# Hybrid encoder on one Trainium2 core: input-projection blocks in another order, the value normalisation's small terms on GpSimd, the convolution's last tile kept in SBUF

## The chip, the cores and the metric

The kernel runs on one core of a Trainium2 chip. The metric is the device time of one execution in microseconds; lower is better. The time before the change is the median of three runs. The hardware profile behind the quoted lines is of one further execution.

A core has five engines that run side by side, each through its own queue in order: TensorE (PE, matrix products; its weight loads are listed as PEld), VectorE (DVE), ScalarE (ACT), GpSimd (POOL) and SyncE (SP), which here only issues transfers. GpSimd issues transfers too: the accumulating ones, which add to a tile in SBUF while they load.

## The reference, cut to what matters

Two layers. Each has a mixer and a gated feed-forward part. The change is in the mixer: one projection, three branches on it, and gates that merge them.

```python
z = xn @ w_in + b_in                       # 1024 positions, 1024 -> 6912
a = zc[..., :768] * sigmoid(zc[..., 768:]) # branch 1
a = dwconv_causal(a, conv_w)               # 31 taps per channel
a = silu(layernorm(a, conv_ln_g, conv_ln_b))
h_a = a @ conv_proj
u, v = split(gelu(zg))                     # branch 2
v = layernorm(v, gmlp_ln_g, gmlp_ln_b)     # then mixed within blocks of 128 positions
h_b = (u * sv) @ gmlp_proj
h_c = multiscale_pool(zp, pool_w, pool_scale) @ pool_proj   # branch 3: windows 2, 4, 8, 16
y = gates[0] * h_a + gates[1] * h_b + gates[2] * h_c        # gates = sigmoid(zgate)
x = x + y @ w_out
```

## The kernel before

**Layout and matrix products.** Channels lie on the 128 partitions, the 1024 positions along the free axis, in two halves of 512. Every float32 operand is split into a rounded part and a remainder (ScalarE casts, VectorE subtracts: `halves`, L343, and `split_to`, L275), and each product is three matmuls of 128x512 (`mms`, L330).

**Blocks.** The input projection has 54 weight tiles of 128 columns. They are taken in pairs, 27 blocks a layer. A block (class `Block`, L364) computes two output tiles `z1` and `z2` over both halves in seven groups of 12 matmuls, a Strassen-like scheme, instead of eight. Its activation operands (`B11`, `B21`, `T2`, `T3`, `T1`, `T4`, `B22`, four buffers each, 28 in all) are made once per layer in `start_phase` (L496) and held through the whole projection. The weight sums that the scheme needs (`s1` to `s4`) are made by accumulating transfers on GpSimd's queue (`more`, L212, and `prepare`, L223), begun nine operands ahead of use. Plain weights (`raw`) are loaded by SyncE, and weights are split three operands ahead (`operand`, L295). `Block.rest` (L392) takes the last four groups: `s3` with `T3`, `s1` with `T1`, plain weights with `T4`, `s4` with `B22`.

**Kinds of blocks.** `glu` blocks give the convolution branch's inputs, `v` and `u` the two parts of branch 2, `zp` the pooling branch, `gate` the gates. `IN_BLOCKS` (L81) is their order, written out by hand. The first four (`EARLY`) share the start phase.

**Background work.** A finished block can append jobs to `background`: a `glu` block one convolution tile (`conv_taps`, L585: 30 steps of one tap on VectorE, and one to sum up the tiles for all but the first), a `v` block two transposed tiles (`transposed`, L646: two steps each), a `zp` block two pooling tiles (`pool_windows`, L607: three to six steps each). `u` and `gate` blocks append nothing; they store their two tiles to DRAM. `pump` (L313) takes a step of the first two jobs in turn. It is called six times a block (four for the first four blocks), with 1.4 steps a call, and 1.8 in the last six blocks. This order is the program's; a planner that places the instructions on the engines' queues at compile time may move them ahead of or behind it, as buffers and its own estimates allow.

**Buffers.** Nearly all tiles of 128x1024 float32 (512 KB, and the operands of the same size) come from one pool of 37 (`slot` and `wide`, L113 and L117). A tile that is stored to DRAM keeps its buffer until the store has landed.

**After the projection.** `mixer_out` (L723) loads the pooled tiles back (`load_pooled`, L714, two transfers of 512 KB each; three of the six tiles in the last block, L701, the others in the loop of L748), mixes them (`mix`), and then runs branch 2 (`spatial`, L769), the convolution's normalisation (`conv_mean`, L823, `conv_norm`, L849) as background work of the three branch projections (`branch`, L873). `spatial` takes the mean and variance of `v` from statistics (`bn`), and makes two tiles of 128x4: `rv`, the inverse root of the variance (an addition on VectorE, L781, and the power on GpSimd, L782), and `nm`, minus the mean times `rv` (VectorE, L784). ScalarE applies them (L786). `conv_mean` loads the six convolution tiles and their sum back from DRAM.

Of the kernel before, what the change touches and what calls it, by code (L numbers as in the profile page):

```python
# [13 lines left out]
P = 128  # L14
# [62 lines left out]
N_PAR = C_LAST + KD  # L77


GATE_BLOCKS = [("gate", j) for j in range(N_GATE // 2)]  # L80
IN_BLOCKS = (  # L81
# [3 lines left out]
    + [("glu", 3)] + GATE_BLOCKS[0:3]  # L85
    + [("glu", 4)] + GATE_BLOCKS[3:6]
    + [("glu", 5)] + GATE_BLOCKS[6:12]
)
EARLY = 4
KEEP = 4  # L90
# [11 lines left out]
def encoder(ctx: ExitStack, tc: tile.TileContext, xt, wts, par, bs, wst, cnt, out):  # L102
# [24 lines left out]
    def half(h):  # L127
        return slice(h * H, (h + 1) * H)
# [184 lines left out]
    def pump(n):  # L313

        state["credit"] = state["credit"] + n if background else 0
        while state["credit"] >= 1 and background:
            job = background.pop(0)
            try:
                next(job)
                state["credit"] -= 1  # L320
                background.insert(1, job)
            except StopIteration:
                pass
# [37 lines left out]
    def add(o, a, b, op=ALU.add):  # L361
        nc.vector.tensor_tensor(o, a, b, op=op)  # L362

    class Block:  # L364
# [24 lines left out]
            self.u2 = temp(f"u2_{self.name}")  # L389
            nc.scalar.copy(self.u2, self.run)  # L390

        def rest(self, dst21, dst22, n_pump=0):  # L392

            key, ops, run, u2 = (self.l, self.ta, self.tb), self.ops, self.run, self.u2
            ps = pm.tile([P, H], F32, tag="mm", name=f"c21_{self.name}")
            mms(ps, operand("s3", key), ops["T3"], True, True)
            p7 = temp(f"p7_{self.name}")
            nc.scalar.copy(p7, ps)  # L398
            pump(n_pump)
            mms(run, operand("s1", key), ops["T1"], False, True, again=True)  # L400
            add(dst22, p7, run, ALU.subtract)
            pump(n_pump)
            mms(ps, operand("raw", (self.l, self.tb, H)), ops["T4"], False, True, again=True)
            add(dst21, ps, u2, ALU.subtract)
            pump(n_pump)
            mms(run, operand("s4", key), ops["B22"], False, True, again=True)
            pump(n_pump)
            return run
# [157 lines left out]
    def mixer_in(l, x0, x1, sq1, ops):  # L566
# [1 line left out]
        tag = f"{l}"  # L568
        d = {
            "gate": [dp.tile([P, S], F32, name=f"gate_{l}_{i}") for i in range(N_GATE)],  # L570
            "conv": [dp.tile([P, S], F32, name=f"convd_{l}_{i}") for i in range(KB)],
            "pooled": [],
            "csum": dp.tile([P, S], F32, name=f"csumd_{l}"),
            "bn": lay.tile([P, S // BLK, KB, 6], F32, tag="bn", name=f"bn_{l}"),
            "u": [dp.tile([P, S], F32, name=f"ud_{l}_{i}") for i in range(KB)],
            "v": dp.tile([P, S // BLK, DB], F32, name=f"vd_{l}"),
# [8 lines left out]
        def conv_taps(i, ain):  # L585
            acc = wide(f"conv_{tag}_{i}")
            w0 = C_CW + i * CONV_K + CONV_K - 1
            nc.scalar.activation(acc, ain, AF.Copy, bias=0.0, scale=col(w0))  # L588
            for k in range(1, CONV_K):
                nc.vector.scalar_tensor_tensor(  # L590
                    acc[:, k:], ain[:, : S - k], col(w0 - k), acc[:, k:],
                    op0=ALU.mult, op1=ALU.add,
                )
                yield
            nc.sync.dma_start(d["conv"][i], acc)

            if i == 0:
                conv_sum.append(acc)
                return
            total = wide(f"csum_{tag}_{i}")  # L600
            add(total, conv_sum.pop(), acc)
            conv_sum.append(total)
            if i == KB - 1:
                nc.sync.dma_start(d["csum"], total)
            yield

        def pool_windows(i, z):  # L607
# [59 lines left out]
        def rest(n, b, n_pump):  # L667
            kind, j = IN_BLOCKS[n]
            z1, z2 = b.z, wide(f"z2_{b.name}")
            ps = b.rest(z2[:, half(0)], z2[:, half(1)], n_pump)  # L670
            if kind == "glu":
                pointwise(z1, ps, AF.Sigmoid, C_BB + j)
                nc.vector.scalar_tensor_tensor(
                    z2, z2, col(C_BA + j), z1, op0=ALU.add, op1=ALU.mult
                )
                background.append(conv_taps(j, z2))
                return
            func, bias = {
                "v": (AF.Gelu_apprx_tanh, C_BV), "u": (AF.Gelu_apprx_tanh, C_BU),
                "zp": (AF.Identity, C_BP), "gate": (AF.Sigmoid, C_BG),  # L680
            }[kind]
            pointwise(z1, ps, func, bias + 2 * j)
            pointwise(z2, None, func, bias + 2 * j + 1)
            for i, z in enumerate((z1, z2)):
                c = 2 * j + i
                if kind == "v":
                    background.append(transposed(c, z))
                elif kind == "zp":
                    background.append(pool_windows(c, z))
                else:  # L690
                    nc.sync.dma_start(d[kind][c], z)
# [31 lines left out]
    def mixer_out(l, d, x_src, x_dst):  # L723
# [45 lines left out]
        def spatial(h):  # L769
# [8 lines left out]
                nc.vector.bn_aggr(mv[:, b, :], d["bn"][:, h * NB + b])  # L778
            yield
            rv = sm.tile([P, NB], F32, tag="rv", name=f"rv_{tag}_{h}")  # L780
            nc.vector.tensor_scalar(rv, mv[:, :, 1], EPS, None, op0=ALU.add)  # L781
            nc.gpsimd.tensor_tensor(rv, rv, mhalf, op=ALU.pow)  # L782
            nm = sm.tile([P, NB], F32, tag="nm", name=f"nm_{tag}_{h}")
            nc.vector.scalar_tensor_tensor(nm, mv[:, :, 0], -1.0, rv, op0=ALU.mult, op1=ALU.mult)  # L784
            for b in range(NB):
                nc.scalar.activation(  # L786
                    v[b][:, :DB], v[b][:, :DB], AF.Identity,
# [33 lines left out]
        conv, squares = [], []  # L821

        def conv_mean():  # L823
            acc = wide(f"csum_{tag}_b")
            reload(acc, d["csum"])
            for i in range(KB):
                c = wide(f"convn_{tag}_{i}")
                reload(c, d["conv"][i])
                conv.append(c)
            yield  # L830
            for h in range(NH):
                sl = half(h)
                mean = pst.tile([P, H], F32, tag="st", name=f"mean_{tag}_{h}")
                nc.tensor.matmul(mean, ones, acc[:, sl], start=True, stop=True)
                sq = None
                for i in range(KB):
                    nc.vector.scalar_tensor_tensor(
                        conv[i][:, sl], mean, -1.0 / DB, conv[i][:, sl], op0=ALU.mult, op1=ALU.add
                    )
                    s = temp(f"csq_{tag}_{h}_{i}")  # L840
                    nc.scalar.activation(s, conv[i][:, sl], AF.Square)
                    if sq is None:
                        sq = s
                    else:
                        add(sq, sq, s)
                    yield
                squares.append(sq)
# [46 lines left out]
                    pump(n_pump)  # L894


        for h in range(NH):
            background.insert(h, spatial(h))
        background.append(conv_mean())
        branch(2, mixed, PUMP[1])  # L900
        drain()
        background.append(conv_norm())
# [289 lines left out]
```

## Time and profile before

| | us |
|---|---|
| median of 3 runs | 2734.74 |
| lowest and highest run | 2734.66, 2737.49 |
| the profiled execution, its own time | 2737.02 |
| its span, first to last instruction | 2735.2 |
| PE busy in the span | 2678.3 |
| DVE busy | 2059.5 |
| ACT busy | 1254.3 |
| POOL busy | 360.6 |

A line of the timeline gives the start, the length, the engine, the line of the kernel, the operation, what it writes `<-` what it reads, the shape, and how many instructions are merged (x12). In square brackets stands how long the engine was idle before it, and what released it. Matmuls are pipelined: the length of a group runs to the modelled end of its last one, so distances between starts are the better measure. A line of the waits gives who waited `<-` for whom: the total in us, how often, and the longest. In a line of stretches the stretch and its length come first, then each engine's busy time, the granted TensorE clock as a share of full speed, the DMA engines' share and GB/s.

In the profiled execution the projection ends and the loop of `mix` begins at 563.5 us in the first layer and at 1907.8 us in the second.

### The profile page before, as it was taken

The page shows a single profiled execution, that of the slowest core. Times are in us where ns is not written, and L with a number is a line of the kernel's source. Part 1 is how long each engine was busy: PE and PEld are TensorE (multiplying, and loading weights), DVE is VectorE, ACT ScalarE, POOL GpSimd, SP SyncE. Part 2 cuts the span into 40 slices and gives each one's busy share as a digit, 9 for nine tenths or more (in the row PEclk, how much of TensorE's full clock was granted, in tenths as well). Part 3 has the DMA queues.
Part 4 walks back from the last instruction along what each step waited for, and adds up shares of the span by engine and source line. Part 5 has one row for each costly group of instructions (what it writes and reads, how often), then busy time and mean ns, then how long its engine had stood idle before and what let it go on. Part 6 is the DMA issues. An engine that isn't in the chain of part 4 may idle for free. (4 is left out here: it accounts for less than half of the span.)

```text
span 2735.2 us, 35037 instructions
## 1 busy us (share of the span) xinstructions
PE 2678.3 (98%) x12122; PEld 2208.2 (81%) x12122; DVE 2059.5 (75%) x2887; ACT 1254.3 (46%) x2047; POOL 360.6 (13%) x411
## 2 busy tenths in 40 slices
PE   6999999999999999999999999999999999999998
PEld 4887888888888788878888878888788888888788
DVE  7988989867756876674579878988676579666656
ACT  5554444443333554453364444444452336445534
POOL 2212111100001221100122111110000022111000
PEclk9999999999999999999999999999999999999999
DMA  9887787684357787665568777876724677774654
GB/s 240 198 216 187 201 230 202 173 281 164 122 177 204 166 209 177 172 203 197 150 149 212 205 206 216 210 208 198 272 81 137 221 181 179 201 182 115 216 179 137
DMA packets 275075, 517.92 MB, mean 189 GB/s; under 512 B 28496, under 2 KB 49744, under 8 KB 274896
## 3 DMA queue, kind: packets, MB, share of 16 engines
q1 hardware_dynamic: 220272, 415.51, 45.8%
q0 software_dynamic: 54624, 100.16, 22.2%
q8 instruction: 95, 1.56, 0.2%
q14 instruction: 84, 0.69, 0.1%
HBM read 385.54 MB, written 89.13 MB: 174 GB/s over the span
## 5 line engine op out<-in xcount | busy, mean ns | idle before, releaser
L287 DVE TENSOR_TENSOR split<-raw,split 128x512 fp32r<-128x512 f32 (+1 forms) x570 | 376.9, 665 | 245.8 <-ACT split L286 238.4
L286 ACT CAST split<-raw 128x512 fp32r<-128x512 f32 (+1 forms) x570 | 342.7, 603 | 465.2 <-PE ph L336 152.3
L590 DVE SCALAR_TENSOR_TENSOR conv<-z_glu,par,conv 128x1017 f32<-128x1017 f32 (+9 forms) x360 | 452.3, 1263 | 10.9 <-ACT conv L588 8.3
L286 ACT CAST split<-s 128x512 fp32r<-128x512 f32 x344 | 213.3, 622 | 363.7 <-issue 120.2
L336 PE MATMUL pd<-h,split 128*128 128x512 f32 (+1 forms) x1536 | 315.1, 364 | 3.4 <-ACT split L286 1.5
L336 PEld LDWEIGHTS pd<-h,split 128*128 128x128 f32 x1536 | 261.9, 188 | 52.0 <-ACT h L358 3.4
L287 DVE TENSOR_TENSOR split<-s,split 128x512 fp32r<-128x512 f32 x344 | 234.9, 686 | 68.2 <-ACT split L286 67.9
L218 POOL DMA_DIRECT2D s<-in_wts_dram x220 | 204.3, 971 | 424.7 <-DMA s<-in_wts_dram 183.6
L218 POOL DMA_DIRECT2D s<-s x156 | 135.9, 871 | 762.5 <-DMA s<-in_wts_dram 290.6
L336 PE MATMUL run_up<-T_f,split 128*128 128x512 f32 x768 | 184.5, 389 | 2.5 <-ACT T_f L345 2.5
L336 PE MATMUL c_up<-T_f,split 128*128 128x512 f32 x768 | 183.8, 389 | 0.3 <-ACT p_up L398 0.3
L336 PE MATMUL run_up<-B_f,split 128*128 128x512 f32 x768 | 182.0, 391 | 2.1 <-DVE upv L362 2.1
L336 PE MATMUL po<-y,split 128*128 128x512 f32 x768 | 175.7, 389 | 0.0
L336 PEld LDWEIGHTS run_up<-B_f,split 128*128 128x128 f32 x768 | 143.4, 188 | 34.2 <-DVE upv L362 4.4
L336 PEld LDWEIGHTS run_up<-T_f,split 128*128 128x128 f32 x768 | 143.8, 188 | 33.4 <-ACT T_f L345 3.4
L336 PEld LDWEIGHTS c_up<-T_f,split 128*128 128x128 f32 x768 | 144.0, 188 | 31.0 <-ACT p_up L398 1.2
L336 PEld LDWEIGHTS po<-y,split 128*128 128x128 f32 x768 | 144.0, 188 | 29.8
L336 PE MATMUL run_gate<-T_m,split 128*128 128x512 f32 x576 | 138.4, 389 | 0.0
L336 PE MATMUL c_gate<-T_m,split 128*128 128x512 f32 x576 | 138.3, 389 | 0.0
L336 PE MATMUL run_gate<-B_m,split 128*128 128x512 f32 x576 | 136.0, 390 | 0.1
L336 PE MATMUL ph<-mixed,split 128*128 128x512 f32 x576 | 135.4, 393 | 0.0
L336 PE MATMUL ph<-us,split 128*128 128x512 f32 x576 | 134.2, 391 | 0.0
(256 smaller groups left out, 4378.3 us busy)
## 6 DMA issues: line engine op xcount, KB each, us to landing
raw<-in_wts_dram SPq DMA_DIRECT2D x518, 256.0 KB, 3.3
s<-in_wts_dram SPq DMA_DIRECT2D x344, 256.0 KB, 3.7
s<-in_wts_dram POOLq DMA_DIRECT2D x220, 256.0 KB, 5.3
s<-s POOLq DMA_DIRECT2D x156, 256.0 KB, 4.2
gate<-z_gate SPq DMA_DIRECT2D x48, 512.0 KB, 4.3
gt<-gate SPq DMA_DIRECT2D x96, 256.0 KB, 3.6
h<-hd SPq DMA_DIRECT2D x56, 256.0 KB, 4.6
pooled_b<-poold SPq DMA_DIRECT2D x24, 512.0 KB, 8.0
```

The lines of the kernel that those rows point to most:

```text
L218: nc.gpsimd.dma_start(s, o, accum_op=ALU.add)
L286: nc.scalar.copy(s[:, 0, :cols], src[:, :cols])
L287: nc.vector.tensor_tensor(s[:, 1, :cols], src[:, :cols], s[:, 0, :cols].bitcast(F32), op=ALU.subtract)
L336: nc.tensor.matmul(ps[:, cols], w[:, i0, wsl], a[:, i1, cols], start=first and k == 0 and j == 0, stop=last and k == n - 1 and j == 2, ski ...
L590: nc.vector.scalar_tensor_tensor(acc[:, k:], ain[:, : S - k], col(w0 - k), acc[:, k:], op0=ALU.mult, op1=ALU.add,)
```

## The change

It has four parts.

1. `IN_BLOCKS` is put in another order. The number and the kinds of blocks are the same. The third `v` block moves into the first four, the three `zp` blocks move back to positions 8, 12 and 16 (from 3, 6 and 9), and the first six gate blocks, which stood three by three behind `glu` 3 and 4, are spread over positions 4, 6, 14, 15, 18 and 19 (counted from 0).
2. In `spatial`, `rv`'s addition and `nm`'s product move from VectorE to GpSimd; `nm`'s one instruction becomes two.
3. `Block.rest` gets a callback `freed`, called after its first, second and third group. In the last block it loads one more pooled tile each time, so that all six are loaded within that block.
4. The last convolution tile and the sum of the tiles stay in SBUF, where they were stored to DRAM and loaded back. `conv_mean` waits for the sum by yielding. `spatial` is appended to the background list where it was inserted at its front.

```diff
+GATES = [("gate", j) for j in range(N_GATE // 2)]
 IN_BLOCKS = (
-    [("glu", 0), ("v", 0), ("v", 1), ("zp", 0)]
-    + [("glu", 1), ("v", 2), ("zp", 1), ("u", 0)]
-    + [("glu", 2), ("zp", 2), ("u", 1), ("u", 2)]
-    + [("glu", 3)] + GATE_BLOCKS[0:3]
-    + [("glu", 4)] + GATE_BLOCKS[3:6]
-    + [("glu", 5)] + GATE_BLOCKS[6:12]
+    [("glu", 0), ("v", 0), ("v", 1), ("v", 2), GATES[0]]
+    + [("glu", 1), GATES[1], ("u", 0), ("zp", 0)]
+    + [("glu", 2), ("u", 1), ("u", 2), ("zp", 1)]
+    + [("glu", 3), GATES[2], GATES[3], ("zp", 2)]
+    + [("glu", 4), GATES[4], GATES[5]]
+    + [("glu", 5)] + GATES[6:12]
 )
...
-        def rest(self, dst21, dst22, n_pump=0):
+        def rest(self, dst21, dst22, n_pump=0, freed=None):
+            freed = freed or (lambda: None)
...
             mms(ps, operand("s3", key), ops["T3"], True, True)
             p7 = temp(f"p7_{self.name}")
             nc.scalar.copy(p7, ps)
+            freed()
             pump(n_pump)
             mms(run, operand("s1", key), ops["T1"], False, True, again=True)
             add(dst22, p7, run, ALU.subtract)
+            freed()
             pump(n_pump)
             mms(ps, operand("raw", (self.l, self.tb, H)), ops["T4"], False, True, again=True)
             add(dst21, ps, u2, ALU.subtract)
+            freed()
             pump(n_pump)
...
-            "conv": [dp.tile([P, S], F32, name=f"convd_{l}_{i}") for i in range(KB)],
+            "conv": [dp.tile([P, S], F32, name=f"convd_{l}_{i}") for i in range(KB - 1)],
-            "csum": dp.tile([P, S], F32, name=f"csumd_{l}"),
...
-            nc.sync.dma_start(d["conv"][i], acc)
+            if i < KB - 1:
+                nc.sync.dma_start(d["conv"][i], acc)
...
             if i == KB - 1:
-                nc.sync.dma_start(d["csum"], total)
+                d["conv_last"], d["csum"] = acc, total
...
-            ps = b.rest(z2[:, half(0)], z2[:, half(1)], n_pump)
+            freed = (lambda: load_pooled(l, d)) if n == len(IN_BLOCKS) - 1 else None
+            ps = b.rest(z2[:, half(0)], z2[:, half(1)], n_pump, freed)
...
-            nc.vector.tensor_scalar(rv, mv[:, :, 1], EPS, None, op0=ALU.add)
+            nc.gpsimd.tensor_scalar(rv, mv[:, :, 1], EPS, None, op0=ALU.add)
             nc.gpsimd.tensor_tensor(rv, rv, mhalf, op=ALU.pow)
             nm = sm.tile([P, NB], F32, tag="nm", name=f"nm_{tag}_{h}")
-            nc.vector.scalar_tensor_tensor(nm, mv[:, :, 0], -1.0, rv, op0=ALU.mult, op1=ALU.mult)
+            nc.gpsimd.tensor_tensor(nm, mv[:, :, 0], rv, op=ALU.mult)
+            nc.gpsimd.tensor_scalar(nm, nm, -1.0, None, op0=ALU.mult)
...
         def conv_mean():
-            acc = wide(f"csum_{tag}_b")
-            reload(acc, d["csum"])
-            for i in range(KB):
+            for i in range(KB - 1):
                 c = wide(f"convn_{tag}_{i}")
                 reload(c, d["conv"][i])
                 conv.append(c)
             yield
+            while "csum" not in d:
+                yield
+            conv.append(d["conv_last"])
+            acc = d["csum"]
...
-        for h in range(NH):
-            background.insert(h, spatial(h))
-        background.append(conv_mean())
+        background.extend([spatial(0), spatial(1), conv_mean()])
```

More of the change, by code (lines that the diff above doesn't have):

```diff
@@ L77 @@
 N_PAR = C_LAST + KD
-GATE_BLOCKS = [("gate", j) for j in range(N_GATE // 2)]
+GATES = [("gate", j) for j in range(N_GATE // 2)]
 IN_BLOCKS = (
[3 rows of a table removed]
-    + [("glu", 3)] + GATE_BLOCKS[0:3]
-    + [("glu", 4)] + GATE_BLOCKS[3:6]
-    + [("glu", 5)] + GATE_BLOCKS[6:12]
+    [("glu", 0), ("v", 0), ("v", 1), ("v", 2), GATES[0]]
[4 more added lines that the diff above has]
+    + [("glu", 5)] + GATES[6:12]
 )
```

## The prediction

> **What bounds the kernel now.** I read the head of the page first, then TensorE's waits, then the stretches around the places that this list names.
>
> ```profile
> span 2735.2 us, 35037 instructions
> PE 2678.3 (98%) x12122; PEld 2208.2 (81%) x12122; DVE 2059.5 (75%) x2887; ACT 1254.3 (46%) x2047; POOL 360.6 (13%) x411
> ...
> PE st_m L416 <- DVE sq_m L362: 13.2, 1, 13.2
> PE run_u L336 <- DVE z_u L362: 8.3, 2, 4.3
> PE mix L336 <- DMA pooled_b<-poold: 2.8, 3, 1.6
> PE sv L797 <- ACT v L786: 0.4, 1, 0.4
> ```
>
> TensorE (PE) is busy 98% of the span, so only 56.9 us of idle time can be won at all, plus whatever its clock loses. The change removes no matmul. The largest wait, st_m at the kernel's start, lies ahead of everything it touches. What it can reach are the run_u and mix waits. The run_u wait comes once per layer:
>
> ```profile
> 250.51 0.61 PE L336 MATMUL c_u<-B_m,split 128*128 128x512 f32 x2
> 255.38 5.49 PE L336 MATMUL run_u<-B_m,split 128*128 128x512 f32 x12 [4.25 <-DVE z_u L362]
> 260.66 2.64 PE L336 MATMUL c_u<-B_m,split 128*128 128x512 f32 x10
> 263.14 2.88 PE L336 MATMUL run_u<-T_m,split 128*128 128x512 f32 x12
> 265.86 2.88 PE L336 MATMUL c_u<-T_m,split 128*128 128x512 f32 x12
> ...
> 1595.21 0.61 PE L336 MATMUL c_u<-B_m,split 128*128 128x512 f32 x2
> 1599.85 5.49 PE L336 MATMUL run_u<-B_m,split 128*128 128x512 f32 x12 [4.03 <-DVE z_u L362]
> 1607.78 2.88 PE L336 MATMUL run_u<-T_m,split 128*128 128x512 f32 x12
> ```
>
> Twelve matmuls take 2.72 us here (263.14 to 265.86). The twelve after the gap took 5.28 (255.38 to 260.66): half speed. So count the loss from start to start: from 250.51 twenty-four matmuls should end 5.44 later, at 255.95; the next group began at 263.14, so 7.19 us are lost, of which 4.25 are idle. In layer 1 it is 1607.78 - (1595.21 + 5.44) = 7.13. Together 14.3 us, although the list of waits shows only 8.3. The granted clock confirms it:
>
> ```profile
> 80.00:231.40 151.40, 151.40 (x689) 125.41 (x688) 140.52 (x210) 77.70 (x123) 30.79 (x35) 1.00 0.83 205
> 231.40:276.70 45.30, 41.05 (x170) 33.40 (x169) 30.05 (x47) 19.21 (x34) 10.13 (x10) 0.92 0.74 202
> 447.50:563.50 116.00, 116.00 (x513) 96.10 (x512) 104.68 (x118) 50.32 (x79) 14.05 (x16) 1.00 0.70 196
> ```
>
> The columns are length, then PE, weight load, VectorE (DVE), ScalarE, GpSimd (POOL), the clock (1.00, in the gap's stretch 0.92) and DMA. Before the gap DVE is busy 140.5 of 151.4 us, 93%, and PE never waits. DVE has little slack there, and what makes it wait is soon passed on to PE.
>
> The Trainium skill, "TensorE: Matmul & The Clock Gate", Part 1, says that the clock falls to half after an idle window of some 3.4 us and returns after as long a busy one. By it a gap costs its idle time and 1.7 us more (half of 3.4): an estimate of 11.7 us for both. The trace's 2.94 and 3.10 beyond the idle time decide.
>
> **Why DVE was late.** DVE's timeline before the late z_u additions, both layers:
>
> ```profile
> 240.31 1.22 DVE L362 TENSOR_TENSOR win<-win 128x1022 f32<-128x1022 f32 x1
> ...
> 242.46 0.16 DVE L784 SCALAR_TENSOR_TENSOR nm<-mv,rv 128x4 f32<-128x4 f32 x1 [0.93 <-POOL rv L782]
> 247.17 0.17 DVE L784 SCALAR_TENSOR_TENSOR nm<-mv,rv 128x4 f32<-128x4 f32 x1 [2.42 <-POOL rv L782]
> 252.89 1.23 DVE L362 TENSOR_TENSOR win<-z_zp 128x1023 f32<-128x1023 f32 x1 [2.33 <-DMA poold<-pooled]
> 254.64 0.68 DVE L362 TENSOR_TENSOR z_u<-p_u,run_u 128x512 f32<-128x512 f32 x1
> ...
> 1587.82 0.17 DVE L784 SCALAR_TENSOR_TENSOR nm<-mv,rv 128x4 f32<-128x4 f32 x1 [0.94 <-POOL rv L782]
> 1591.85 0.16 DVE L784 SCALAR_TENSOR_TENSOR nm<-mv,rv 128x4 f32<-128x4 f32 x1 [1.73 <-POOL rv L782]
> 1597.38 1.22 DVE L362 TENSOR_TENSOR win<-z_zp 128x1023 f32<-128x1023 f32 x1 [2.13 <-DMA poold<-pooled]
> ```
>
> DVE waited 0.93 + 2.42 + 2.33 = 5.68 us for a 4.25 us gap on PE, and 0.94 + 1.73 + 2.13 = 4.80 us for 4.03. So PE absorbs 0.8 to 1.4 us and gets the rest. Two causes stand side by side: the round trip to GpSimd's power, and a pooling window that waits for a buffer until the store of a pooled tile has landed.
>
> **The change, part by part.** *Value terms on GpSimd.*
>
> ```profile
> L786 ACT ACTIVATE v<-v,nm,rv x16: 1011/1014/1030, 591.6 to 1945.0; 128x768 f32<-128x768 f32 x16
> L781 DVE TENSOR_SCALAR rv<-mv x4: 93/136/165, 240.3 to 1588.6; 128x4 f32<-128x4 f32 x4
> L782 POOL TENSOR_TENSOR rv<-rv,mhalf x4: 1352/1644/1947, 240.5 to 1590.5; 128x4 f32<-128x4 f32 x4
> L138 POOL MEMSET mhalf<- 128x4 f32 x1 | 0.1, 102 | 0.0
> ```
>
> The planner has moved rv and nm some 350 us ahead of their reader (first starts 240.3 and 591.6), into the middle of the input projection. The edit takes 4 rv and 4 nm off DVE: 4 x 0.14 + 4 x 0.16 = 1.2 us busy, and above all the waits, 3.35 us in layer 0 and 2.67 in layer 1. GpSimd gets three instructions more per half, 12 in all, each between 0.10 us (its memset of the same shape) and 1.64 us (its power): 1.2 to 19.7 us in all. I take about 0.3 each, near the memset, since plain arithmetic isn't a power. Behind them in GpSimd's queue stand the accumulating DMAs of the weight sums; one half can hold them back by 0.3 to 4.9 us. GpSimd is busy 10.1 of 45.3 us there and the sums are begun nine operands (9 x 2.72 = 24 us) before use, so I cost that at nothing; without that cover it is at most 4.9 us per half.
>
> A rule speaks against the move: the Trainium skill, "GPSIMD Engine Reference", section 1, says that GpSimd shares its SBUF interface with VectorE and that instructions with two SBUF inputs contend. What that would do is a rival below.
>
> *Order of the blocks.* No block is added or dropped; the total of background steps is the same (185 convolution, 12 value, 28 pooling steps), and both orders leave one step at the end. What changes is how many 512 KB buffers of the shared pool of 37 are held. Stepping through pump() for both orders, with 28 held by the projection's operands: the old order wants 38 at blocks 7, 8, 10, 11 and 13 (counted from 0), and the gap is at the end of block 10, where a window waits for a buffer. The new order wants at most 37, at blocks 4 (the old order wants 37 there as well) and 18, where the last pooling tiles now are, and 33 to 36 elsewhere. The count leaves out how long stores hold a buffer:
>
> ```profile
> poold<-pooled SPq DMA_DIRECT2D x12, 512.0 KB, 5.1
> gate<-z_gate SPq DMA_DIRECT2D x48, 512.0 KB, 4.3
> csumd<-csum SPq DMA_DIRECT2D x2, 512.0 KB, 3.3
> csum_b<-csumd SPq DMA_DIRECT2D x2, 512.0 KB, 6.3
> ```
>
> So at block 18 a wait between 0 and 5.1 us (a whole store) is possible. I take about 1, under what PE absorbs, since the old order's waits came only above 37. With both causes gone, both gaps go: 14.3 us. Next late is nothing that the list of waits shows in this stage.
>
> *Loads of the pooled tiles into freed operand buffers.*
>
> ```profile
> 568.13 4.50 SPq L201 DMA_DIRECT2D pooled_b<-poold  x6
> ...
> 563.52 9.68 PE L336 MATMUL mix<-pooled_b,split 128*128 128x512 f32 x42
> 573.99 0.93 PE L336 MATMUL mix<-pooled_b,split 128*128 128x512 f32 x3 [0.78 <-DMA pooled_b<-poold]
> 575.34 9.12 PE L336 MATMUL mix<-pooled_b,split 128*128 128x512 f32 x39 [0.42 <-DVE mixed L759]
> ...
> 1919.10 0.93 PE L336 MATMUL mix<-pooled_b,split 128*128 128x512 f32 x3 [1.59 <-DMA pooled_b<-poold]
> 1920.45 9.09 PE L336 MATMUL mix<-pooled_b,split 128*128 128x512 f32 x39 [0.42 <-DMA pooled_b<-poold]
> ...
> DMA to landing us min/median/max: 4.9/8.7/11.0
> ```
>
> Six loads (three tiles) go out at 568.13 for matmuls that were due at 573.2. The edit puts them behind the last block's T3, T1 and T4 groups: mix begins at 563.52, three groups of 2.72 after T3's end, so from about 555.4 on. With 11.0 us to land they are there by about 569. Waits removed: 0.78 + 1.59 + 0.42 = 2.8 us; the 0.42 for DVE stays. The price: SyncE's queue waits for those groups, and the weight loads for mix queue behind by at most one group, 2.72 us; they are split several us ahead of use, so nothing. Bounds of this part: 3.2 us gained to 5.4 lost.
>
> *Last convolution tile and sum in SBUF.* Per layer two stores and two loads of 512 KB go. No PE wait names them, so nothing is gained. Two buffers stay held until conv_mean; the value loads could come later, and PE's one wait for them is 0.4 us. Bounds: 0.4 gained, 3.3 (a store's time) lost per layer; I take 0. The changed place of spatial() in the background list does nothing, as the list is empty by then.
>
> **The sum.** 14.3 + 2.8 = 17.1 us. The profiled execution took 2737.02 us, 1.8 more than its span; it becomes about 2719.9, the span 2718.1. The median of the runs before, 2734.74, is 0.08% under the profiled one, and becomes 2717.6. The three runs spread over 2.8 us, so 0.2% (5.5 us) is about what can be told from no change.
>
> **Rivals.**
> *Half of it:* GpSimd's round trip goes but the buffer wait stays. PE's gaps shrink to 4.25 - 3.35 = 0.90 and 4.03 - 2.67 = 1.36 us. A gap of 1.59 us (at 1919.10) was followed by full speed, so no clock is lost: 2.3 us more, 2719.9. This lies inside my own range.
> *The gap moves:* the static order puts an equal stall elsewhere in each layer, likeliest at blocks 17 to 19, where 37 of 37 buffers are wanted and two gate stores of 4.3 us each lie between. Price 14.3 us: 2731.9, no difference that can be told. For it: DVE is 90% busy in the last blocks (104.7 of 116). Against: there, too, PE never waited. That the edits leave the waits where they are comes to the same time. Chance 0.17.
> *Slower:* both pooling tiles of that pair wait for a store at the same place, behind gate stores in SyncE's queue; each holds DVE a whole 5.1 us, and the faster tap rate of the last six blocks leaves no slack between. Each stall is then about a gap of 4 us and 3 us of half clock. Four such cost 28.6: 2746.2. It decides against the change from 17.1 us, 8.6 per layer. For it: that pair has moved next to those blocks. Against: the old order's pair ran beside gate blocks as well, and PE's list of waits names no z_gate. Chance 0.10.
> *GpSimd slows DVE:* if DVE stands still while the 12 added instructions run at their upper 1.64 us, and PE sees all of it, 19.7 us return: 2737.3, within 0.2%. Against: the window addition that ran beside the first power (both start at 240.3 to 240.5) took 1.22 us, and those with no power beside them 1.22 and 1.23 (252.89, 1597.38). Chance 0.03, shared between same and slower.
>
> **How the numbers follow.** Forecast with the half case 0.70, its own range 2714 (the remaining 0.4 + 0.4, and the spread) to 2722 (half case plus 2). To 2736 the range takes in the moved gap and leaves out the slower case and edges, under 0.2. Faster by over 0.2% (under 2729.3): 0.70. Same: 0.17 and part of the last, 0.18. Slower: 0.12.
>
> **What would show it.** Right: no run_u or other PE wait over 2 us between 80 and 565 us and in the same part of layer 1, the clock 1.00 throughout; no DVE wait for POOL rv; mix without a pooled_b wait. Wrong: a PE wait for a z_ addition at another block, a DVE win wait over 2 us at blocks 16 to 19, or s sums landing late behind GpSimd's new instructions.

## The result, and the profile after

| | before | after |
|---|---|---|
| first comparison, median us (runs) | 2736.11 (4) | 2721.73 (4) |
| second comparison, the same kernel again | 2733.84 (9) | 2718.73 (5) |
| ratio, 95% interval: first | | 0.9943 [0.9932, 0.9955] |
| ratio, 95% interval: second | | 0.9944 [0.9931, 0.9956] |
| profiled execution, span | 2735.2 | 2719.7; second one 2714.3 |

The change makes the kernel faster by 0.57%, about 15.5 us; the interval allows 12 to 19. The forecast was 17.1 us, and the time forecast, 2717.6, stands 1.1 us below the second median and 4.1 below the first.

The head of the page after the change, with its busy times, and the line of PE's waits that has grown:

```profile
PE 2671.9 (98%) x12122; PEld 2206.4 (81%) x12122; DVE 2058.4 (76%) x2879; ACT 1254.6 (46%) x2047; POOL 370.2 (14%) x423
...
PE sv L806 <- ACT v L795: 2.1, 3, 1.1
```

The lines for run_u on z_u and for mix on pooled_b are gone; the one for sv (branch 2 mixing the values `v`, which come back from DRAM, over positions) has grown from 0.4 to 2.1. DVE's busy time is 1.1 us less and POOL's 9.6 more. (Line numbers have shifted: L336 is now L337, L782 now L790.) PE's timeline where the gap of layer 0 was, and the first two stretches again, around that place:

```profile
245.67 2.88 PE L337 MATMUL c_u<-T_m,split 128*128 128x512 f32 x12
248.39 5.60 PE L337 MATMUL run_u<-B_m,split 128*128 128x512 f32 x24
253.83 2.88 PE L337 MATMUL c_u<-B_m,split 128*128 128x512 f32 x12
```

```profile
80.00:231.40 151.40, 151.40 (x690) 125.36 (x689) 142.59 (x214) 76.14 (x120) 37.47 (x42) 1.00 0.83 211
231.40:276.70 45.30, 45.30 (x201) 37.53 (x200) 32.91 (x40) 23.88 (x37) 7.91 (x9) 1.00 0.84 231
```

Twenty-four matmuls take 5.44 us, start to start (248.39 to 253.83). PE is busy throughout both stretches at clock 1.00. In the first stretch POOL has 6.7 us more than before, since the value terms of both halves now lie there. The mix follows without a gap (the first nine of its 84 matmuls already stand ahead of the projection's last group, at 553.03), and the new wait comes behind it:

```profile
557.89 17.16 PE L337 MATMUL mix<-pooled_b,split 128*128 128x512 f32 x75
574.89 12.40 PE L337 MATMUL ph<-mixed,split 128*128 128x512 f32 x54
...
588.74 1.94 PE L806 MATMUL sv<-ws,v 128*128 128x128 f32 x18 [0.78 <-ACT v L795]
```

```profile
1927.54 1.94 PE L806 MATMUL sv<-ws,v 128*128 128x128 f32 x18 [1.12 <-ACT v L795]
```

**A ruler for the stage.** Whole times scatter by several us from run to run, so the kernels are also compared by one stretch of PE's timeline: the last 2150 matmuls ahead of the first `ph` (the branch projections) of a layer, counted one by one in the trace, from about 91 us to the end of mix in layer 0 and the same in layer 1. Before the change they took 492.93 us in layer 0 and 493.31 in layer 1. After it they took 482.92 in both, in the second profile 482.93 and 482.91. So 10.0 + 10.4 = 20.4 us went. The stretch from the first `ph` to the first `po` (the product with `w_out`) grew by 1.08 and 1.02 (213.39 to 214.47, 214.26 to 215.28), in the second profile by 0.07 and not at all.

The rest of the difference between the spans lies in code that the change does not touch. The feed-forward's first product of layer 0 (first `run_up` to first `pd`) took 310.52 us before, 312.33 and 310.18 in the two profiles after, and 309.5 to 312.8 over all the kernels below. The matmuls of layer 0 ahead of the ruler, from the first `run_glu` on, took 70.68 before, 70.99 and 71.14 after, and 70.6 to 74.5 below. One run of the kernel with the loads alone, 3361.23 us at a granted clock of 0.753 where its other runs had 0.995 to 0.997, lies far off all others and is left out of its ratio.

### The profile page after: what moved, and what is told of

Read it like the earlier page. It is cut to its first block, busy times and chain, and to the rows that moved or that the text cites. A ratio compares the mean times of both kernels' runs of the same rounds, so it can differ in the third digit from the quotient of the medians.

```text
span 2719.7 us, 35012 instructions
## 1 busy us (share of the span) xinstructions
PE 2671.9 (98%) x12122; PEld 2206.4 (81%) x12122; DVE 2058.4 (76%) x2879; ACT 1254.6 (46%) x2047; POOL 370.2 (14%) x423
## 4 chain that ended last, share of the span: by engine, by line
PE 81%; issue 13%; DVE 3%; DMA 2%; ACT 1%; POOL 0%; SPq 0%; DVEq 0%; POOLq 0%; ACTq 0%
PE run_up L337 13%; PE pd L337 12%; PE run_gate L337 10%; PE c_up L337 9%; PE c_gate L337 7%; PE run_glu L337 5%; PE ph L337 4%; PE c_glu L337 4%; PE po L337 3%; PE run_zp L337 2%; PE run_u L337 2%; PE run_v L337 2%; PE c_u L337 2%; PE c_zp L337 2%; PE c_v L337 1%
## 5 line engine op out<-in xcount | busy, mean ns | idle before, releaser
L595 DVE SCALAR_TENSOR_TENSOR conv<-z_glu,par,conv 128x1011 f32<-128x1011 f32 (+7 forms) x360 | 452.5, 1264 | 7.3 <-ACT conv L593 4.5
L337 PE MATMUL pd<-h,split 128*128 128x512 f32 (+1 forms) x1536 | 314.7, 364 | 3.7 <-ACT split L287 1.5
L337 PEld LDWEIGHTS pd<-h,split 128*128 128x128 f32 x1536 | 262.2, 189 | 51.9 <-ACT h L359 3.5
L337 PE MATMUL run_up<-T_f,split 128*128 128x512 f32 x768 | 184.5, 389 | 2.5 <-ACT T_f L346 2.5
L337 PE MATMUL run_up<-B_f,split 128*128 128x512 f32 x768 | 183.4, 393 | 2.5 <-DVE upv L363 2.5
L337 PE MATMUL c_up<-T_f,split 128*128 128x512 f32 x768 | 183.8, 389 | 0.3 <-ACT p_up L401 0.3
L337 PE MATMUL po<-y,split 128*128 128x512 f32 x768 | 175.7, 389 | 0.0
L337 PEld LDWEIGHTS run_up<-B_f,split 128*128 128x128 f32 x768 | 144.2, 189 | 34.8 <-DVE upv L363 4.7
L337 PEld LDWEIGHTS run_up<-T_f,split 128*128 128x128 f32 x768 | 143.8, 188 | 33.4 <-ACT T_f L346 3.5
L337 PEld LDWEIGHTS c_up<-T_f,split 128*128 128x128 f32 x768 | 144.0, 188 | 31.1 <-ACT p_up L401 1.2
L337 PEld LDWEIGHTS po<-y,split 128*128 128x128 f32 x768 | 144.0, 188 | 29.8
L337 PE MATMUL c_gate<-T_m,split 128*128 128x512 f32 x576 | 138.6, 389 | 0.0
L337 PE MATMUL run_gate<-T_m,split 128*128 128x512 f32 x576 | 138.5, 389 | 0.0
L337 PE MATMUL run_gate<-B_m,split 128*128 128x512 f32 x576 | 136.3, 389 | 0.0
L337 PE MATMUL ph<-mixed,split 128*128 128x512 f32 x576 | 136.1, 394 | 0.0
L337 PE MATMUL ph<-us,split 128*128 128x512 f32 x576 | 134.2, 391 | 0.0
```

Of the source, the lines that this page charges most:

```text
L337: nc.tensor.matmul(ps[:, cols], w[:, i0, wsl], a[:, i1, cols], start=first and k == 0 and j == 0, stop=last and k == n - 1 and j == 2, ski ...
L595: nc.vector.scalar_tensor_tensor(acc[:, k:], ain[:, : S - k], col(w0 - k), acc[:, k:], op0=ALU.mult, op1=ALU.add,)
```

## Experiments

The four parts are called order, GpSimd, loads and SBUF. Each table row gives the median, the ratio to the kernel before in its own comparison, and the ruler. The kernel before had 2737.17 us in the comparison with the four parts alone, 2734.21 in that with the two kernels that leave out SBUF or the loads, and 2733.84 in that of the other rows.

| parts in the kernel | us | ratio [95%] | last 2150 matmuls, L0 / L1 |
|---|---|---|---|
| none (before) | | 1 | 492.93 / 493.31 |
| GpSimd | 2729.50 | 0.9970 [0.9959, 0.9981] | 487.86 / 488.05 |
| order | 2729.43 | 0.9976 [0.9967, 0.9986] | 489.68 / 487.41 |
| loads | 2732.71 | 0.9981 [0.9972, 0.9990] | 489.61 / 490.04 |
| SBUF | 2733.84 | 0.9987 [0.9978, 0.9997] | 491.67 / 490.11 |
| order, GpSimd | 2720.56 | 0.9954 [0.9942, 0.9967] | 484.75 / 484.25 |
| GpSimd, loads, SBUF | 2724.19 | 0.9960 [0.9946, 0.9973] | 486.28 / 486.53 |
| order, GpSimd, loads | 2718.89 | 0.9951 [0.9938, 0.9963] | 482.92 / 482.91 |
| order, GpSimd, SBUF | 2718.41 | 0.9949 [0.9936, 0.9963] | 483.70 / 483.70 |
| all | 2718.73 | 0.9944 [0.9931, 0.9956] | 482.93 / 482.91 |

(In the kernels with SBUF and without loads the planner sets four `mean` matmuls ahead of the first `ph`, inside the ruler. Each takes 0.43 us where the others take 0.23; take 0.8 us off there.)

### GpSimd alone

```diff
-            nc.vector.tensor_scalar(rv, mv[:, :, 1], EPS, None, op0=ALU.add)
+            nc.gpsimd.tensor_scalar(rv, mv[:, :, 1], EPS, None, op0=ALU.add)
...
-            nc.vector.scalar_tensor_tensor(nm, mv[:, :, 0], -1.0, rv, op0=ALU.mult, op1=ALU.mult)
+            nc.gpsimd.tensor_tensor(nm, mv[:, :, 0], rv, op=ALU.mult)
+            nc.gpsimd.tensor_scalar(nm, nm, -1.0, None, op0=ALU.mult)
```

> The kernel before with the value terms on GpSimd alone; order, loads and stores as before. If both causes add up (my theory): the DVE waits for POOL rv go, the wait for poold stays, PE's gap shrinks from 4.25 and 4.03 us to about 0.9 and 1.4 with the clock staying at 1.00: 12 us faster than before, about 2724. If the buffers decide and the round trip to GpSimd is harmless: the gaps stay over 3 us with the clock dip, no difference, 2736. If the round trip alone makes the gap: no gap over 0.3 us, 14.3 us faster, 2722.

The gaps shrank to 2.14 and 2.25 us, not to 0.90 and 1.36. DVE's and PE's timelines of this kernel at the place:

```profile
247.70 0.69 DVE L287 TENSOR_TENSOR split<-s,split 128x512 fp32r<-128x512 f32 x1 [1.32 <-ACT split L286]
250.88 1.23 DVE L362 TENSOR_TENSOR win<-z_zp 128x1023 f32<-128x1023 f32 x1 [2.49 <-DMA poold<-pooled]
```

```profile
250.60 0.61 PE L336 MATMUL c_u<-B_m,split 128*128 128x512 f32 x2
253.36 3.03 PE L336 MATMUL run_u<-B_m,split 128*128 128x512 f32 x12 [2.14 <-DVE z_u L362]
256.23 2.43 PE L336 MATMUL c_u<-B_m,split 128*128 128x512 f32 x10
```

DVE no longer waits for GpSimd, and the window addition starts at 250.88 instead of 252.89: 2.01 us earlier, where 3.35 us of waits had gone. The freed time met two other waits. The split waits 1.32 us for ScalarE (0.17 before), and the store's landing, which the window waits for, came late enough to make that wait 2.49 instead of 2.33. 3.35 - 1.15 - 0.16 = 2.04. The gap on PE shrank by the same, 4.25 - 2.14 = 2.11. And after a gap of 2.14 us the next twelve matmuls took 2.87 (253.36 to 256.23): no half clock. The ruler gained 5.07 and 5.26.

### Order alone

```diff
-    [("glu", 0), ("v", 0), ("v", 1), ("zp", 0)]
-    + [("glu", 1), ("v", 2), ("zp", 1), ("u", 0)]
...
+    [("glu", 0), ("v", 0), ("v", 1), ("v", 2), GATES[0]]
+    + [("glu", 1), GATES[1], ("u", 0), ("zp", 0)]
...
```

> The kernel before with the new order of blocks alone; rv and nm stay on VectorE. If both causes add up: no DVE wait for poold, but the wait for the power remains, some 3 to 4 us, now at an earlier block; PE absorbs 0.8 to 1.4 of it and shows a gap of 2 to 3 us without loss of clock: 14.3 - 2 x 2.5 = 9 us faster, about 2727. If the order alone decides: no gap, 14 us faster, 2722. If the round trip alone makes the gap: it moves with nm, over 3.4 us with the clock dip, no difference, 2736.

No window waits for a store in this kernel, and there is no gap at run_u. New gaps stand at another block, 80 us earlier. GpSimd, DVE and PE:

```profile
163.60 0.88 POOL L218 DMA_DIRECT2D s<-s  x1 [6.93 <-DMA s<-in_wts_dram]
164.16 2.36 POOL L782 TENSOR_TENSOR rv<-rv,mhalf 128x4 f32<-128x4 f32 x2
```

```profile
165.57 0.16 DVE L784 SCALAR_TENSOR_TENSOR nm<-mv,rv 128x4 f32<-128x4 f32 x1 [5.54 <-POOL rv L782]
166.55 0.16 DVE L784 SCALAR_TENSOR_TENSOR nm<-mv,rv 128x4 f32<-128x4 f32 x1 [0.82 <-POOL rv L782]
```

```profile
169.24 3.01 PE L336 MATMUL run_gate<-T_m,split 128*128 128x512 f32 x12 [2.29 <-ACT u_gate L390]
172.09 2.88 PE L336 MATMUL c_gate<-T_m,split 128*128 128x512 f32 x12
176.62 3.06 PE L336 MATMUL run_gate<-B_m,split 128*128 128x512 f32 x12 [1.66 <-DVE z_gate L362]
```

With the third `v` block in the first four, the statistics are complete at some 160 us instead of 240, and the planner sets the value terms there. At that point an accumulating DMA on GpSimd's queue is waiting 6.93 us for the load that it adds to. The power stands behind it in order, and DVE stands 5.54 us behind the power. Both powers together take 2.36 us once they run; it isn't the power that is slow. So the order by itself trades one stall of DVE for another; the ruler gained 3.25 and 5.90.

### Order and GpSimd together, and everything but the order

The first kernel has the two diffs above. The second has GpSimd, loads and SBUF, with the old `IN_BLOCKS`.

> Only the new order and the GpSimd edit. Theory (the gap needs both, and they do not add): no wait of PE at a z_u, u_gate or z_gate addition over 1 us between 80 and 565 us or in the same part of layer 1, so the whole 14.3 us go, where the two singly brought 7 to 8 us each and left gaps of 1.7 to 2.3 us. The waits of mix on its pooled tiles stay (before: 0.78 + 0.42 in layer 0, 1.59 + 0.42 in layer 1) because the store of the sum still stands in SyncE's queue: about 2 to 3 us over the kernel with all parts, 2720 to 2724. Rival (the loads or the kept sum take part in removing the gap): a gap of 1 us or more stays at one of these places, 2724 or more.

> All parts but the new order of the blocks. Theory (the order is needed for what the GpSimd edit leaves): the wait of VectorE's window addition for the store of a pooled tile stays, with a gap of PE of about 2.1 and 2.3 us at run_u as in the kernel with the GpSimd edit alone; mix does not wait. About 4.4 us over the kernel with all parts: 2724 to 2727. Rival (the old order is as good once GpSimd has the value terms and the sum stays in SBUF): no gap over 1 us, time within 2 us of the kernel with all parts.

With both, PE has no wait between 80 us and the mix of layer 0, and one of 0.2 us between 1400 us and the mix of layer 1. The waits for the pooled tiles remain, one line for each layer's stretch:

```profile
PE mix L336 <- DMA pooled_b<-poold: 1.4, 2, 1.0
```

```profile
PE mix L336 <- DMA pooled_b<-poold: 0.9, 2, 0.5
```

The ruler gained 8.18 + 9.06 = 17.2 us of the 20.4. The two parts alone gained 10.3 and 9.2, together 19.5. That counts the half clock twice: either part alone brings it back, 2.94 + 3.10 = 6.0 us. Without it the two gained 4.3 and 3.1 alone and 11.2 together, since each alone leaves DVE waiting at a point that the other also touches.

With the old order the gaps stay, at 1.34 and 1.84 us:

```profile
251.88 1.23 DVE L362 TENSOR_TENSOR win<-z_zp 128x1023 f32<-128x1023 f32 x1 [1.06 <-DMA poold<-pooled]
```

```profile
255.09 3.02 PE L336 MATMUL run_u<-B_m,split 128*128 128x512 f32 x12 [1.34 <-DVE z_u L362]
257.94 2.43 PE L336 MATMUL c_u<-B_m,split 128*128 128x512 f32 x10
```

```profile
1597.45 4.59 PE L336 MATMUL run_u<-B_m,split 128*128 128x512 f32 x12 [1.84 <-DVE z_u L362]
1601.88 2.43 PE L336 MATMUL c_u<-B_m,split 128*128 128x512 f32 x10
```

By the ruler, the order is worth 3.4 and 3.6 us in the full kernel (486.28 and 486.53 against 482.93 and 482.91). The medians say 5.5 us on the same chip, with intervals that overlap.

### Loads alone, SBUF alone

```diff
             nc.scalar.copy(p7, ps)
+            freed()
...
+            freed = (lambda: load_pooled(l, d)) if n == len(IN_BLOCKS) - 1 else None
```

```diff
-            nc.sync.dma_start(d["conv"][i], acc)
+            if i < KB - 1:
+                nc.sync.dma_start(d["conv"][i], acc)
...
-                nc.sync.dma_start(d["csum"], total)
+                d["conv_last"], d["csum"] = acc, total
```

> The kernel before with the last three pooled tiles loaded within the last block alone. As predicted: no PE wait for pooled_b at mix, 2.8 us less than before, about 2733.3, and sv starts with no more wait than before (0.4 us in layer 1). If SyncE's queue, waiting for TensorE's groups, holds the weight loads back: a new PE wait for a split at mix, and 0 to 2 us slower. If the sv wait of the changed kernel comes from these loads: sv waits 0.8 and 1.3 us here too, and the gain is about 1 us.

> The kernel before with the last convolution tile and the sum kept in SBUF alone. As predicted: no difference, 2736. If the sv wait of the changed kernel comes from the two held buffers (in SyncE's queue one weight load now stands ahead of the v loads): sv waits for ACT v about 1 us in each layer, where before it was 0 and 0.4, so 1 to 2 us slower, about 2737.5. If that wait belongs to the other parts: sv as before.

In both, mix waits for nothing, and both gained more than was expected (by their ratios 5.2 us where 2.8 stood, and 3.6 where nothing stood). For the loads that was the aim. For SBUF it was not foreseen: I had costed it at nothing. SyncE's queue shows why, first before the change with the wait of that queue (the late six loads follow, at 568.13), then in the SBUF kernel:

```profile
567.72 0.33 SPq L604 DMA_DIRECT2D csumd<-csum  x1
```

```profile
SPq L604 <- DVE csum L362: 1.6, 1, 1.6
```

```profile
565.75 4.25 SPq L201 DMA_DIRECT2D pooled_b<-poold  x6
```

The store of the sum stood ahead of the late pooled loads in SyncE's order, so they could go out only once DVE had made the sum. Without that store they go out 2.4 us earlier (2.0 by the distance from the start of mix), and land in time for mix. So two parts of the change remove the same wait. The gaps at run_u stay in both, with the half clock behind them (the loads kernel, whose gap was 3.76):

```profile
254.87 5.49 PE L336 MATMUL run_u<-B_m,split 128*128 128x512 f32 x12 [3.76 <-DVE z_u L362]
260.15 2.74 PE L336 MATMUL c_u<-B_m,split 128*128 128x512 f32 x10
```

### Without SBUF, without loads

All parts but one, in each case.

> The changed kernel without its fourth part: the last convolution tile and the sum go to DRAM and back as before. In the changed kernel PE waits 0.8 and 1.3 us for v at sv. If the two held buffers make that wait (one weight load stands ahead of the v loads in SyncE's queue): sv waits 0.4 us or less, and it is 1 to 2 us faster than the changed kernel, about 17 us under the kernel before. If the wait comes from the third part (mix no longer stalls, so its end comes sooner after the loads): sv waits as in the changed kernel and the time is the same.

> The changed kernel without its third part: three of the six pooled tiles are loaded after the last block, as before. The fourth part alone had taken mix's wait away, by taking the store of the sum out of SyncE's queue ahead of the loads. If that is the cause: no PE wait for pooled_b here either, and the same time as the changed kernel within 1 us. If the early loads are needed: mix waits 0.8 to 2 us per layer, 2 to 3 us slower than the changed kernel.

Without SBUF, sv waits 0 and 0.2 us; without the loads it doesn't wait at all. Both have no wait of mix. SyncE's queue after the change, before it, and without SBUF, at the value loads:

```profile
577.19 0.33 SPq L194 DMA_DIRECT2D raw<-in_wts_dram  x1
577.58 5.05 SPq L202 DMA_DIRECT2D v<-vd  x8
```

```profile
584.84 5.89 SPq L201 DMA_DIRECT2D v<-vd  x8
```

```profile
578.85 5.81 SPq L201 DMA_DIRECT2D v<-vd  x8
```

After the change the value loads stand behind a weight load that waits for a buffer, and go out 2.7 us after the first `ph` (577.58 against 574.89). Without SBUF they go out 1.2 us after it (578.85, `ph` at 577.61), before the change 0.5 (584.84, `ph` at 584.30). The reader, sv, comes 12.2 us behind the first `ph` (574.89 to 587.13 after the change), whatever the loads do. Without the loads the values stand behind the weight load too, 2.7 us after the first `ph` (578.39 against 575.71), and yet sv doesn't wait. The difference is in the landing: ScalarE starts on the first value 4.7 us after the issue there (583.05), 5.9 after it in the first profile of the change (583.46), and again 4.7 in its second (576.81 to 581.50). So SBUF, together with the new place in the queue, seems to use up the lead of the value loads, and what sv then waits depends on how fast they land in that run. That SBUF is the cause is not shown: with SBUF alone the values stand behind a weight load too, and sv doesn't wait. In the time it does not show: 2718.89 and 2718.41 against 2718.73 for all parts.

### Value loads earlier, one buffer fewer

In the first kernel the loop of mix stands behind the filling of the background list, with all parts kept; the second of the kind leaves the loads out as well. The third takes one buffer from the pool.

```diff
         background.extend([spatial(0), spatial(1), conv_mean()])
+        for m in range(KB):
+            mine = [n for n, (_, mm) in enumerate(POOL_PAIRS) if mm == m]
...
+            pump(1)
         branch(2, mixed, PUMP[1])
```

```diff
-N_SLOTS, N_TT, N_S, N_RAW, N_SPLIT = 37, 6, 8, 5, 5
+N_SLOTS, N_TT, N_S, N_RAW, N_SPLIT = 36, 6, 8, 5, 5
```

> The changed kernel with the background list filled before the mix loop, so that the v loads are issued during mix. If the late issue of the v loads makes sv wait: no wait at sv, 2 us faster than the changed kernel, the fastest of all. If the loads collide: mix or its weight splits wait for DMA, and nothing is gained or 1 to 3 us lost.

> All parts but the early loads of the pooled tiles, and the background list filled ahead of the loop of mix, so that the value loads are issued earlier. Theory: no mix wait (the store of the sum is out of SyncE's queue), no sv wait; 2716 to 2720, 2 us under the kernel with all parts. Rival (the waits at sv are taken up elsewhere): within 1 us of the kernel with all parts, whatever sv shows.

> The changed kernel with 36 buffers in the shared pool where it has 37. By my count of buffers it wants 37 at blocks 4 and 18. If buffers pace the projection: DVE or ACT wait over 2 us for a store there, and PE shows a gap of 1.5 to 5 us in each layer, 4 to 14 us slower than the changed kernel. If the count means little: under 1 us.

The first values went out 13 us ahead of the first `ph` (564.18 against 577.38), and sv had no wait in either kernel:

```profile
564.18 0.96 SPq L202 DMA_DIRECT2D v<-vd  x2
```

The times were 2719.47 (0.9953 [0.9939, 0.9967]) and 2719.13 us (0.9944 [0.9932, 0.9957]), no better than all parts. The ruler stood at 482.91 / 482.92, and at 483.69 / 483.69 with the `mean` matmuls inside it. The second profile of the kernel with all parts had only 0.5 us of sv waits in all, so there was little to win.

With 36 buffers the time was 2718.81 (0.9948 [0.9936, 0.9961]), the ruler 483.19 / 483.18. DVE's waits in the projection of layer 0 show that buffers are now short, and PE's that it doesn't matter:

```profile
DVE win L363 <- DMA poold<-win: 1.3, 1, 1.3
...
DVE z_gate L363 <- DMA poold<-pooled: 0.9, 1, 0.9
```

They come at 414.5 and 411.9 us, in block 19. Neither reaches PE; the 0.27 us that the ruler has more lie ahead of both, at 404.96. A larger pool wasn't tried.

### All parts once more

> The kernel with all parts once more, beside its variants on one chip. Theory: two or three waits of sv on ScalarE's v, some 2 us in all, no run_u and no mix wait; 2719 to 2723, and 1 to 3 us over the kernel without the early loads. Rival: the sv wait does not show in the time, both within 1 us.

It had 2718.73 us, and one sv wait of 0.5 us. So the sv waits of 2.1 us in the first profile are not a fixed property of the kernel, and the rival expectation, that they don't show in the time, holds as far as these runs can tell.

## Why the prediction was right, and where not

**The gap at run_u, 14.3 us: right.** Both idle gaps and the half clock behind them are gone, and no stall of their size turned up elsewhere. The likeliest case came in, with 482.9 us for 2150 matmuls in both layers.

**The causes: two, as said, but coupled otherwise than said.** The text on record treated the waits as terms that can be struck out one by one. GpSimd alone left 2.14 and 2.25 us of gap and not 4.25 - 3.35 and 4.03 - 2.67, because the wait for a split and the landing of a store took up 1.3 of the 3.35 us. That subtraction is the step of the half case that failed. It also missed what the order needs from the GpSimd edit. The power meets the accumulating DMAs in GpSimd's queue. The prediction asked only how long the new instructions hold the DMAs back, and not how long a DMA holds the power back. Before the change that was already the larger part of the round trip. The addition of the second half was done at 243.42, but GpSimd's queue stood at an accumulating DMA, and the power began only at 245.78:

```profile
243.26 0.16 DVE L781 TENSOR_SCALAR rv<-mv 128x4 f32<-128x4 f32 x1
```

```profile
245.15 0.92 POOL L218 DMA_DIRECT2D s<-s  x1 [2.72 <-ACT win L628]
245.78 1.36 POOL L782 TENSOR_TENSOR rv<-rv,mhalf 128x4 f32<-128x4 f32 x1
```

(What that DMA waited for is put down to ScalarE here, and in layer 1 to the load that it adds to, 2.04 us.) Those 2.36 us are nearly the whole of DVE's wait of 2.42; in layer 1 it is 1.66 of 1.73 (addition done at 1588.80, power from 1590.46). After the change the same wait is there, and nobody is hurt by it:

```profile
163.90 0.89 POOL L219 DMA_DIRECT2D s<-s  x1 [6.99 <-DMA s<-in_wts_dram]
164.86 1.10 POOL L789 TENSOR_SCALAR rv<-mv 128x4 f32<-128x4 f32 x1
166.04 1.33 POOL L790 TENSOR_TENSOR rv<-rv,mhalf 128x4 f32<-128x4 f32 x1
...
173.19 0.94 POOL L219 DMA_DIRECT2D s<-in_wts_dram  x1
```

The reader of nm is ScalarE, some 420 us later; DVE has left the chain.

**GpSimd's twelve instructions: mis-sized, without effect.** Taken at 0.3 us each; the medians of rv's addition, nm's product and its sign are 0.80, 0.34 and 0.84. Both halves hold the queue from 164.86 to 173.19, 8.3 us. No matmul of the projection waits for a weight sum, so the nine operands of lead covered it, as said.

**GpSimd slows DVE: did not happen.** Two of DVE's taps, the first begun while the first power runs (166.04 to 167.37) and the second beside nm's product and sign, and the same two in the order kernel, where none of these runs beside them:

```profile
166.38 2.59 DVE L595 SCALAR_TENSOR_TENSOR conv<-z_glu,par,conv 128x1021 f32<-128x1021 f32 x2
```

```profile
171.59 2.59 DVE L590 SCALAR_TENSOR_TENSOR conv<-z_glu,par,conv 128x1021 f32<-128x1021 f32 x2
```

They take the same 2.59 us. The rule of the Trainium skill, "GPSIMD Engine Reference", section 1, on contention is not seen here with four elements a partition.

**The order by the count of buffers: right in place, not in price.** The prediction set the border at the size of the pool: waits above, none up to it. With 37 in the pool the new order shows no such wait. With 36 it shows DVE waits of 1.3 and 0.9 us in block 19, next to block 18, where the count wants 37, none at block 4, where it wants 37 as well, and no loss on PE from them. That the old order makes windows wait for stores and the new one doesn't is shown by the traces (2.49 and 1.06 us for pooled tiles in the two kernels with the old order and the GpSimd edit, and 1.0 to 2.5 for stores of `u` tiles; none with the new order). That the count of buffers alone decides it is not shown, and stays open. The stalls given a chance at blocks 16 to 19 did not come: at full pool no window waited there.

**Mix, 2.8 us: right in place, too small.** Before the change the three matmuls from 573.99 to 575.34 took 1.35 us start to start, of which 0.67 are matmuls and 0.42 is listed as idle; 0.26 more is lost in filling the pipeline again. Over the whole of mix: its 84 matmuls should take 19.0 us at 2.72 for twelve, and took 20.8 in layer 0 (563.52 to 584.30) and 21.5 in layer 1 (1907.84 to 1929.37), so 1.7 + 2.5 = 4.2 us were lost. With the 14.3 that is 18.5 of the 20.4; another 0.6 lay at a z_glu wait in layer 0, and the rest in pieces under 0.3 us.

**SBUF, taken at 0: wrong in mechanism, near in time in the full kernel.** It removes the mix wait by itself, which the queue's order would have told: the store of the sum stood one line ahead of the late loads. And sv waited 2.1 us over both layers in one profile with it, inside the bound of 3.3 per layer that was given; in others with it sv waited 0, 0.5 and 1.1 us. In the full kernel one of the two parts is enough; neither costs nor brings anything that can be told.

**The sum.** 17.1 forecast, about 15.5 measured. By the first profile's stage it is 20.4 - 2.1 = 18.3, by the second's 20.4 - 0.1 = 20.3; the interval of 12 to 19 holds the former and not the latter. That the forecast came so near is in part luck: the terms that it left out or took too small come to some 3 us by the ruler, and the whole times gained 3 to 5 us less than the ruler. Part of this may be the one profile before the change, whose execution took 2737.02 us, 0.9 and 3.2 over the medians of the two comparisons: in the kernels with loads or SBUF alone, which leave run_u as it was, 13.9 and 13.3 us were lost there and not 14.3. What the remaining difference is, beyond the scatter of untouched stages, isn't settled.

## What to carry to other kernels

When two waits stand one behind the other on an engine, taking one away gives back only what the next fixed point in time (a landing, another engine's result) leaves. Look up where each would have ended by itself before subtracting. When an edit moves a chain in time, look at what stands ahead of it on every queue at the new place: a computing instruction behind a DMA issue that waits for data inherits that wait. And a store that waits for a late result blocks the loads queued behind it, so keeping a tile in SBUF can pay through SyncE's order and not through its bytes.

## What the hardware showed that was not expected

**When the clock falls.** Gaps of 1.34, 2.14 and 2.29 us were followed by full speed (twelve matmuls in 2.85 to 2.87 us), those of 3.76 and 4.25 by half speed (5.28). But one gap of 1.84 us, in layer 1 with the old order, was followed by slow matmuls: twelve in 4.43 us (1597.45 to 1601.88 above). And a gap of 5.31 us, in layer 1 of the loads kernel, was followed by half speed for a shorter time than that of 4.25. In these traces the half clock comes in stretches of 3.41 us: two of them in each layer before the change, one in each of the other two cases. So cut, rows of stretches show PE's busy time (the figure behind the length) and the clock (the third from the end), before the change, in the loads kernel, and with the old order:

```profile
250.77:254.18 3.41, 0.35 (x2) 0.00 (x0) 1.29 (x2) 1.20 (x3) 0.00 (x0) 1.00 0.82 301
254.18:257.59 3.41, 2.21 (x5) 1.82 (x6) 2.34 (x4) 1.15 (x1) 0.95 (x1) 0.50 0.35 91
257.59:261.00 3.41, 3.41 (x9) 2.64 (x8) 0.00 (x0) 0.10 (x1) 0.00 (x0) 0.50 0.96 271
```

```profile
1595.40:1598.81 3.41, 0.00 (x0) 0.00 (x0) 2.27 (x3) 1.19 (x3) 0.00 (x0) 1.00 0.60 217
1598.81:1602.22 3.41, 3.20 (x8) 2.53 (x9) 1.35 (x3) 1.15 (x1) 0.92 (x1) 0.50 0.54 103
```

```profile
1594.50:1597.91 3.41, 1.57 (x7) 0.99 (x7) 2.99 (x4) 1.24 (x3) 0.00 (x0) 1.00 0.71 202
1597.91:1601.33 3.42, 3.42 (x10) 2.64 (x9) 0.68 (x2) 1.15 (x1) 0.87 (x1) 0.50 0.55 115
```

A stretch in which PE was busy for 0 to 1.57 us was followed by one at half clock. One at half clock was followed by another where PE was busy for 2.21 us of it, and by full speed where it was busy for 3.20 or more. The gap of 1.84 us lies whole in one stretch. The gap of 2.14 in the kernel with GpSimd alone lies across two, if the stretches are counted back from that kernel's next half clock, at 1190.49; PE was busy for 1.88 us of the second (251.82 to 255.24), and the clock held. Where the border lies is not shown: in the order kernel a stretch with 1.54 us (165.41 to 168.83, counted back from 2718.59) cost no clock. So the length of a single gap doesn't decide alone; where it falls among the stretches seems to count as well. The Trainium skill, "TensorE: Matmul & The Clock Gate", Part 1, ties the clock to a window of about 3.4 us that runs freely, and says that it falls after an idle one. The length agrees with the 3.41 us here. A gap of 1.84 us cannot fill such a window, so by its words this clock should have held; the measurement decides. The prediction's own bound, that a gap of 1.59 us costs no clock, rested on one case.

**Small work on GpSimd.** The same instruction on four elements a partition took from 0.24 to 1.11 us (rv's addition), the power 1.33 to 2.13; spans on this engine are rough. What cost time, before the change and in the order kernel, was not these but the 2.0 to 6.9 us that its queue stood at an accumulating DMA ahead of the power.
